# A two-layer hybrid decoder trunk: the projection for the state-space mixer is handed out ahead of the convolution's

## The chip, the cores and the metric

The kernel runs on one core of a Trainium2 chip. The metric is the device time of one execution in microseconds (us). Three runs of the kernel before took 914.29, 914.33 and 915.61 us, a median of 914.33 us. All arithmetic is done on two layers, a sequence of 512 tokens and a model width of 1024.

## The reference, cut to what matters

```python
for layer in range(DEPTH):                       # 2 layers
    h = rms_norm(x, norm_g[layer])
    proj = h @ w_in[layer]                       # 1024 x 5120, ten column blocks of 512
    a_u, a_g, qd, kd, vd, b_g, c_x, c_g, m_q, m_g = jnp.split(proj, 10, axis=-1)
    y_a = s5_mixer(a_u, ...)                     # complex state space, GELU, then a GLU (w_glu)
    o_b = diff_attention(rope(qd), rope(kd), vd) # 4 heads, causal, two softmaxes each
    y_c = rglru_mixer(c_x, ...)                  # width-4 causal convolution, gates, a linear recurrence
    y_m = memory_attention(m_q, rms_norm(mem), w_mem_kv[layer])   # 256 memory tokens
    mixed = concat(y_a * silu(a_g), norm(o_b) * silu(b_g), y_c * silu(c_g), y_m * silu(m_g))
    x = x + mixed @ w_out[layer]                 # 2048 x 1024
return rms_norm(x, final_norm_g)
```

The ten blocks of `proj` depend on `h` alone, so they may be computed in any order. Each mixer can start once its own blocks are there.

## The kernel before, in words

**Weights.** All weights are cut into 136 pieces of 128 x 1024 numbers. A piece is loaded by SyncE into one of two `raw` buffers, and then split into two reduced-precision halves: ScalarE rounds it to `whi` (line 166), VectorE computes `wlo = raw - whi` (line 172). TensorE multiplies each piece three times (hi by hi, hi by lo, lo by hi; lines 517 and 537), 24 matmuls of 512 columns for one piece of `w_in`. There are three `whi` and three `wlo` buffers, and the split of a piece is handed out two pieces ahead of its use (`w_use`, line 176). A full block of 512 output columns is four pieces.

**The order.** `ORDER` (line 31) names for each layer the sequence of the projections; `kv` stands for the memory's keys and values, `gl` for the GLU, the last four for the output projection. The main loop (from line 1155 on) goes through this list. The blocks `q`, `k`, `v` and `au` are computed with the tokens on the partitions (`tm_block`), the others with the channels there (`cm_block`), in two halves `u = 0, 1`.

**Streams and steps.** Beside the main loop run the mixers, as Python generators that hand out a few instructions at a time. After every 12 weight matmuls (half a piece) `tick` (line 78) advances a counter, and each generator that is due hands out its next portion. I call one advance a step. A block of four pieces is 8 steps, `kv` is 12. Counting from the start of a layer, `q k v` and their like fix when a mixer starts:

- `attention` (line 610) starts once q, k and v are there, and hands out one of 16 items (a block of 128 queries, one head) every 2 steps. Its VectorE work is a maximum, some small operations and one combination (lines 652 to 664), and a split of the queries (`ql`).
- the evacuation of `cx` (line 1187) does the convolution: three VectorE operations for each of four column groups. After it `lru` (line 724) starts: for each of four groups a split (`xh`, `xl`), six matmuls with the four gate matrices `bh`, `bl` (lines 740 to 742), then products, a square root and a scan (lines 747, 754, 760).
- `s5` (line 927) starts after `au`: four steps that transpose u to `U`, then for each of four groups f of state columns, every 7 steps (`D_S5`, line 55): `states` (matmuls into the PSUM tile `sc`), `turned` (line 1017: six table products and six products that rotate the states, five tiles `u tcq tsq xr0 xr1`), `scans` (line 1046), `w_rows`, `turned_back`, `c_weights`, `w_turn`. It ends with four steps that make `yhi` and `ylo`, which `gl` needs: at `gl` the main loop joins the stream (line 1250).
- gates (`cg bg ag mg`) are evacuated by ScalarE and VectorE (lines 719, 720).

**What else sets the order.** The instructions of an engine are placed by a planner at build time, with what was handed out first having priority. Buffers of one pool are given out in the order in which their first writers were handed out. The pools that matter: 14 large tiles (`big`, line 97: whole activations such as `kT`, `U`, `xc`, the gates), 10 small tiles of 2 KB a partition (`sm2`, line 99: every working tile of attention, `lru` and `s5`), and in PSUM four `acc`, two `tp` and one `sc`; `sc` is shared by the scores of both attentions and by `states`. The gate matrices of `lru` occupy four small tiles from their loading on; `lru_load` (line 1126, GpSimd DMAs) is called when `cx` is at most two items ahead (`BD_AHEAD`, line 52).

Of the kernel before, what the change touches and what calls it, by code (L numbers as in the profile page):

```python
# [27 lines left out]
ROPE_THETA = 500000.0  # L28


ORDER = ["q v k kv cx au cg bg mq ag mg gl oAM0 oAM1 oBC0 oBC1".split(),
         "q k cx v kv au mq bg mg ag cg gl oAM0 oAM1 oBC0 oBC1".split()]

C_ID, C_DM, C_IF, C_KEEP, C_CM, C_END = 0, 128, 144, 152, 152, 280

# [55 lines left out]
def tile_kernel(ctx: ExitStack, tc: tile.TileContext, A, out):  # L91
# [127 lines left out]
    for l in range(DEPTH):  # L219
        for n in ORDER[l]:  # L220
            if n == "kv":
# [900 lines left out]
    def run_split(g, R):  # L1122
        for _ in split_mixed(R[{"A": "ag", "B": "bg", "C": "cg", "M": "mg"}[g]], R, g):
            pass
# [24 lines left out]
    def s5p_start(l):  # L1149
        s5_load(l, Rl[l])  # L1150
        st.start("s5p", s5_params(l, Rl[l]))
# [3 lines left out]
    for pi, (l, n, u, ids) in enumerate(plan):  # L1155
# [118 lines left out]
        if n == "o":  # L1274
            pair, half = u[:2], int(u[2])
            tile_of = {"A": "ag", "B": "bg", "C": "cg", "M": "mg"}
            waits = {"A": ("s5",), "B": ("bfin", "attn"), "C": ("cfin", "lru"), "M": ("mem",)}
            first = "o" + u == ORDER[l][-4]
            if first:
# [6 lines left out]
            for g in pair:  # L1286
                if half == 0 and g not in R:
                    st.join(*waits[g])
                    run_split(g, R)
            if half == 1 and "o" + u == ORDER[l][-3]:  # L1290
                def nextsplit(R=R, gs=ORDER[l][-2][1:3]):
                    for g in gs:
                        while any(w in st.live for w in waits[g]):
                            yield
                        yield from split_mixed(R[tile_of[g]], R, g)
                st.start("nextsplit", nextsplit())
            if "o" + u == ORDER[l][S5P_AT - 4] and l + 1 < DEPTH:
                s5p_start(l + 1)
            if "o" + u == ORDER[l][-2]:
                st.join("nextsplit")  # L1300
# [74 lines left out]
```

## Time and profile before

| | |
|---|---|
| median of three runs | 914.33 us |
| the profiled execution's own time | 913.18 us |
| its span (first to last instruction of the program) | 911.4 us |
| TensorE busy (matmul) | 890.5 us, 98% of the span |
| TensorE weight loads | 748.9 us, 82% |
| VectorE busy | 658.8 us, 72% |
| ScalarE busy | 509.6 us, 56% |
| GpSimd busy | 42.1 us, 5% |
| granted TensorE clock | 0.998 |
| HBM traffic | 88.6 MB, 97 GB/s |

The share of an engine over the span is a mean over stages with different limits; the stretches below are read one by one. A matmul's recorded duration is longer than the distance to the next matmul's start, since matmuls overlap in the array, so busy TensorE is not TensorE at its peak.

### The profile page before, as it was taken

What the parts mean: (1) busy time and instruction counts of PE and PEld (TensorE: products, weight loads), DVE (VectorE), ACT (ScalarE), POOL (GpSimd) and SP (SyncE); (2) the same over time, 40 slices, a digit from 0 to 9 for tenths busy, and PEclk for the clock granted to TensorE, in tenths of its full rate; (3) what the DMA queues carried; (4) which work ended last, traced back from release to release, by engine and by line L of the source; (5) the groups of instructions that cost most, each with busy time, mean ns of one, the idle gap of its engine ahead of it and who ended that gap; (6) DMA issues with size and microseconds to landing.
All of it is one profiled execution on the core that took longest, in us unless ns stands there. A gap on an engine that the chain in (4) does not pass through costs nothing.

```text
span 911.4 us, 12490 instructions
## 1 busy us (share of the span) xinstructions
PE 890.5 (98%) x4542; PEld 748.9 (82%) x4542; DVE 658.8 (72%) x1315; ACT 509.6 (56%) x1031; POOL 42.1 (5%) x86
## 2 busy tenths in 40 slices
PE   8999999999999999999999999999999999999996
PEld 5788888978878888888888888898888888788885
DVE  6985888678999856983474667764899996666343
ACT  6764887985434265922554568766655344863133
POOL 1001000001110100000100000000101110000000
PEclk9999999999999999999999999999999999999999
DMA  5733432212222237432343332432112222152322
GB/s 185 196 118 102 140 93 70 70 47 72 75 70 61 75 104 205 135 111 93 127 140 92 93 93 70 137 95 70 51 47 83 63 74 93 47 185 98 108 72 93
DMA packets 80930, 90.07 MB, mean 99 GB/s; under 512 B 23778, under 2 KB 58211, under 8 KB 80868
## 3 DMA queue, kind: packets, MB, share of 16 engines
q1 hardware_dynamic: 77842, 85.72, 30.3%
q10 hardware_dynamic: 722, 2.36, 0.8%
q0 software_dynamic: 2304, 1.18, 0.5%
q8 instruction: 36, 0.59, 0.3%
q14 instruction: 26, 0.21, 0.1%
HBM read 84.40 MB, written 4.19 MB: 97 GB/s over the span
## 4 chain that ended last, share of the span: by engine, by line
PE 72%; DVE 18%; ACT 6%; issue 2%; DMA 1%; SPq 0%; DVEq 0%; ACTq 0%
PE acc L537 37%; PE acc L517 17%; PE acc L1261 5%; DVE wlo L172 2%; DVE u L347 2%; DVE xr L1046 2%; DVE wt L347 2%; PE ms L682 1%; DVE xr L347 1%; PE tp L312 1%; PE sc L810 1%; PE tp L1012 1%; PE sc L647 1%; PE sc L648 1%; ACT whi L166 1%
## 5 line engine op out<-in xcount | busy, mean ns | idle before, releaser
L172 DVE TENSOR_TENSOR wlo<-raw,whi 128x1024 fp32r<-128x1024 f32 x136 | 166.2, 1222 | 125.3 <-ACT whi L166 121.6
L166 ACT CAST whi<-raw 128x1024 fp32r<-128x1024 f32 x136 | 143.1, 1052 | 194.1 <-PE acc L537 120.1
L517 PE MATMUL acc<-hThi,whi 128*128 128x512 f32 x384 | 154.3, 402 | 0.0
L517 PE MATMUL acc<-hThi,wlo 128*128 128x512 f32 x384 | 151.1, 394 | 0.0
L517 PE MATMUL acc<-hTlo,whi 128*128 128x512 f32 x384 | 150.6, 392 | 0.0
L537 PE MATMUL acc<-whi,hThi 128*128 128x512 f32 x256 | 104.1, 407 | 1.0 <-ACT whi L166 1.0
L537 PE MATMUL acc<-wlo,hThi 128*128 128x512 f32 x256 | 100.7, 393 | 0.0
L537 PE MATMUL acc<-whi,hTlo 128*128 128x512 f32 x256 | 100.7, 394 | 0.0
L537 PE MATMUL acc<-wlo,mxh 128*128 128x512 f32 x256 | 100.2, 391 | 0.0
L537 PE MATMUL acc<-whi,mxh 128*128 128x512 f32 x256 | 100.1, 391 | 0.0
L537 PE MATMUL acc<-whi,mxl 128*128 128x512 f32 x256 | 100.1, 391 | 0.0
L517 PEld LDWEIGHTS acc<-hThi,wlo 128*128 128x128 f32 x384 | 72.2, 188 | 15.0
L517 PEld LDWEIGHTS acc<-hTlo,whi 128*128 128x128 f32 x384 | 72.4, 189 | 13.4
L517 PEld LDWEIGHTS acc<-hThi,whi 128*128 128x128 f32 x384 | 72.4, 189 | 13.0
L537 PEld LDWEIGHTS acc<-whi,hThi 128*128 128x128 f32 x256 | 56.3, 220 | 9.1 <-ACT whi L166 1.4
L537 PEld LDWEIGHTS acc<-whi,hTlo 128*128 128x128 f32 x256 | 56.1, 219 | 7.8 <-DVE hTlo L315 0.2
L537 PEld LDWEIGHTS acc<-wlo,hThi 128*128 128x128 f32 x256 | 56.4, 220 | 7.1
L537 PEld LDWEIGHTS acc<-whi,mxl 128*128 128x128 f32 x256 | 48.1, 188 | 9.8
L537 PEld LDWEIGHTS acc<-wlo,mxh 128*128 128x128 f32 x256 | 48.1, 188 | 9.7
L537 PEld LDWEIGHTS acc<-whi,mxh 128*128 128x128 f32 x256 | 48.1, 188 | 9.6
L982 POOL DMA_DIRECT2D MT<-kq x64 | 32.1, 509 | 490.7 <-DVE kq L347 339.4
L658 ACT ACTIVATE e<-sc,nmx 128x128 f32<-128x128 f32 (+3 forms) x64 | 33.1, 524 | 7.1 <-DVE nmx L654 5.8
(316 smaller groups left out, 1642.2 us busy)
## 6 DMA issues: line engine op xcount, KB each, us to landing
raw<-in_w_in_dram SPq DMA_DIRECT2D x80, 512.0 KB, 3.7
raw<-in_w_out_dram SPq DMA_DIRECT2D x32, 512.0 KB, 3.3
raw<-in_w_mem_kv_dram SPq DMA_DIRECT2D x16, 512.0 KB, 3.3
x<-in_x_dram SPq DMA_DIRECT2D x8, 512.0 KB, 4.7
raw<-in_s_w_glu_dram SPq DMA_DIRECT2D x16, 256.0 KB, 3.1
mt<-in_mem_dram SPq DMA_DIRECT2D x4, 512.0 KB
xd<-x SPq DMA_DIRECT2D x4, 512.0 KB, 4.0
x<-xd SPq DMA_DIRECT2D x4, 512.0 KB, 5.6
```

Of the source, the lines that this page charges most:

```text
L166: S.copy(hi, wbuf[j])
L172: V.tensor_tensor(out=lo, in0=raw, in1=hi, op=ALU.subtract)
L312: lastins["pe"] = PE.transpose(pt[:, k, :], h[:, kk * 128:(kk + 1) * 128], ident)
L347: V.tensor_tensor(out=o, in0=a, in1=b, op=op)
L517: PE.matmul(a[j][:, :ncol], w[:, kk, c], h(k), start=(hf == 0 and i == 0), stop=(hf == 1 and i == 3 * nh - 1))
L537: PE.matmul(a[t], h(k, t), w[:, kk, :], start=(p == 0 and kk == 0 and i == 0), stop=(p == np_ - 1 and kk == 1 and i == 2))
L647: PE.matmul(s[:, m, :M], qh[:, m, h, :], kT[m][:, h, :M], start=True, stop=False)
L648: PE.matmul(s[:, m, :M], ql[:, m, h, :], kT[m][:, h, :M], start=False, stop=False)
L658: S.activation(e[:, m, :N], s[:, m, :N], AF.Exp, bias=nmx[:, m:m + 1], scale=0.125, accum_out=sm[:, m:m + 1])
L982: G.dma_start(out=MT[g * 64 + 64 - n:g * 64 + 64, g, t], in_=kq[g * 64:g * 64 + n])
L1046: V.tensor_tensor_scan(out=xr_[i][:, j, :], data0=dec, data1=xr_[i][:, j, :], initial=0.0, op0=ALU.mult, op1=ALU.add)
L1261: PE.matmul(a, w[:, k, s, j * 128:(j + 1) * 128], h[:, 2 * hf + k, :], start=(hf == 0 and i == 0), stop=(hf == 1 and i == 5))
```

## The change

```diff
-ORDER = ["q v k kv cx au cg bg mq ag mg gl oAM0 oAM1 oBC0 oBC1".split(),
-         "q k cx v kv au mq bg mg ag cg gl oAM0 oAM1 oBC0 oBC1".split()]
+ORDER = ["q v k kv au cx cg bg mq ag mg gl oAM0 oAM1 oBC0 oBC1".split(),
+         "q k v kv au cx mq bg mg ag cg gl oAM0 oAM1 oBC0 oBC1".split()]
```

In the first layer `au` and `cx` change places. In the second layer `cx` moves from the third place to the one behind `au`, so `v`, `kv` and `au` each come one block (8 steps) sooner. Nothing else differs: the same pieces are loaded and multiplied, and the same mixers run. The steps at which the mixers' portions are handed out, counted from the start of each layer, follow from the code:

| portion | layer 1 before | after | layer 2 before | after |
|---|---|---|---|---|
| attention, items 0 to 15 | 25 to 55 | 25 to 55 | 33 to 63 | 25 to 55 |
| `cx` (convolution) | 36 to 44 | 44 to 52 | 16 to 24 | 44 to 52 |
| `lru`, gate matmuls | 45 to 48 | 53 to 56 | 25 to 28 | 53 to 56 |
| `lru`, the rest | 49 to 58 | 57 to 66 | 29 to 38 | 57 to 66 |
| `s5`, `U` | 53 to 56 | 45 to 48 | 53 to 56 | 45 to 48 |
| `s5`, first `w_rows`, first `turned` | 57, 59 | 49, 51 | 57, 59 | 49, 51 |
| `s5`, last `scans` | 82 | 74 | 82 | 74 |
| `s5`, `yhi` complete | 89 | 81 | 89 | 81 |
| memory attention, from | 93 | 93 | 77 | 77 |
| `gl`, from | 92 | 92 | 92 | 92 |

## Rows read from the trace of the kernel before

**Rows 1.** The page: busy us (share of span), engine by engine.
```profile
PE 890.5 (98%) x4542; PEld 748.9 (82%) x4542; DVE 658.8 (72%) x1315; ACT 509.6 (56%) x1031; POOL 42.1 (5%) x86
```
**Rows 2.** Busy time by stretch: us from the start, length, each engine's busy us (instructions).
```profile
117.00:147.00 30.00, 29.55 (x158) 24.65 (x157) 25.08 (x48) 21.88 (x61) 0.00 (x0) 1.00 0.36 106
147.00:184.00 37.00, 37.00 (x184) 34.51 (x184) 25.43 (x42) 32.59 (x68) 0.00 (x0) 1.00 0.18 57
184.00:207.00 23.00, 21.98 (x125) 17.87 (x124) 17.93 (x27) 17.70 (x32) 0.00 (x0) 1.00 0.16 47
207.00:303.00 96.00, 94.00 (x517) 80.03 (x517) 92.10 (x175) 40.57 (x84) 16.04 (x32) 1.00 0.25 75
303.00:335.00 32.00, 31.26 (x157) 26.01 (x156) 21.89 (x40) 15.76 (x21) 0.00 (x0) 1.00 0.26 83
...
593.00:643.00 50.00, 49.72 (x259) 45.37 (x259) 29.57 (x52) 32.00 (x76) 0.00 (x0) 1.00 0.24 74
643.00:750.00 107.00, 106.07 (x608) 90.31 (x607) 102.42 (x196) 54.34 (x122) 16.05 (x32) 1.00 0.22 68
```
**Rows 3.** The same, for the weight split on VectorE (line 172) alone.
```profile
207.00:303.00 96.00, 14.64 (x12) 1.00 0.25 75
643.00:750.00 107.00, 14.57 (x12) 1.00 0.22 68
```
**Rows 4.** The chain of waits between 207 and 303 us, shares by line.
```profile
by line: DVE u L347 14.0%; DVE wlo L172 10.9%; DVE wt L347 10.3%; DVE xr L347 8.4%; DVE xr L1046 7.7%; issue 6.9%; DVE tcq L347 5.2%; DVE xp L347 4.7%; PE acc L517 4.7%; DVE tsq L347 4.1%; DVE VV L347 3.0%; DVE bg L720 2.7%; DVE cg L765 2.4
```
**Rows 5.** TensorE instructions in time: start us, duration us.
```profile
187.90 0.83 PE L682 MATMUL ms<-v,pT 128*128 128x128 f32 x6
...
223.11 0.39 PE L517 MATMUL acc<-hThi,whi 128*128 128x512 f32 x1
223.34 0.39 PE L517 MATMUL acc<-hTlo,whi 128*128 128x512 f32 x1
...
726.64 1.59 PE L810 MATMUL sc<-kv,qm 128*128 128x256 f32 x12
```
**Rows 6.** VectorE instructions in time, inside the state-space part.
```profile
281.99 0.67 DVE L347 TENSOR_TENSOR wt<-apr,bbx 128x512 f32<-128x512 f32 x1
282.58 0.69 DVE L347 TENSOR_TENSOR wt<-api,bby 128x512 f32<-128x512 f32 x1
```
**Rows 7.** Groups of instructions, both layers: convolution, recurrence; busy us, mean ns.
```profile
L1187 DVE SCALAR_TENSOR_TENSOR xc<-cx,pv,xc 128x509 f32<-128x509 f32 (+2 forms) x24 | 18.0, 749 | 3.4 <-ACT xc L1185 3.0
L760 DVE TENSOR_TENSOR_SCAN li<-lr,xc 128x512 f32<-128x512 f32 x8 | 9.6, 1212 | 0.0
L747 DVE SCALAR_TENSOR_TENSOR xc<-li,xc 128x512 f32<-128x512 f32 x8 | 5.5, 691 | 2.6 <-ACT li L743 2.5
L347 DVE TENSOR_TENSOR xl<-xc,xh 128x512 fp32r<-128x512 f32 x8 | 5.5, 686 | 0.5 <-ACT xh L735 0.5
L754 DVE SCALAR_TENSOR_TENSOR li<-a,li 128x512 f32<-128x512 f32 x8 | 5.4, 686 | 1.5 <-ACT a L753 1.4
L347 DVE TENSOR_TENSOR xc<-xc,li 128x512 f32<-128x512 f32 x8 | 5.3, 682 | 4.5 <-ACT li L756 4.5
```
**Rows 8.** Attention's VectorE groups between 147 and 207 us.
```profile
L652 DVE TENSOR_REDUCE mx<-sc 128x2 f32<-128x1024 f32 (+1 forms) x6 | 6.8, 1133 | 3.5 <-PE sc L650 3.5
L664 DVE SCALAR_TENSOR_TENSOR e<-e,cc 128x512 f32<-128x512 f32 (+1 forms) x7 | 4.9, 694 | 0.2
L347 DVE TENSOR_TENSOR ql<-qT,qh 64x512 fp32r<-64x512 f32 x4 | 2.7, 685 | 0.1
L663 DVE TENSOR_SCALAR cc<-sm,nlam,rc 128x1 f32<-128x1 f32 x7 | 1.9, 270 | 0.2
```
**Rows 9.** The reduction of memory attention, both layers.
```profile
L812 DVE TENSOR_REDUCE mmx<-sc 128x4 f32<-128x1024 f32 x8 | 9.8, 1223 | 4.9 <-PE sc L810 4.9
```
**Rows 10.** Tile U between 150 and 330 us: its writer, first and last start.
```profile
L935 ACT COPY U<-tp x4: 562/603/638, 196.2 to 202.8; 128x512 f32<-128x512 f32 x4
```
**Rows 11.** Loads on the queues: count, KB each, median us from issue to landing.
```profile
raw<-in_w_in_dram SPq DMA_DIRECT2D x80, 512.0 KB, 3.7
bd<-in_lru_w_a_dram POOLq DMA_DIRECT2D x4, 64.0 KB, 2.3
```

## The prediction

> **What bounds the kernel now.** I read the page's busy shares first, then the stretches, then the chain of waits of one stretch. The shares say TensorE: 98% busy against 72% of VectorE [rows 1]. The stretches show that this hides two regimes. From 147 to 184 us TensorE is busy all the time and VectorE only 25.43 of 37 us. From 207 to 303 us VectorE is busy 92.10 of 96 us, and from 643 to 750 us 102.42 of 107 [rows 2]. These two stretches are steps 57 to about 83 of the layers, the state-space part from its first `w_rows` to its last `scans`. That TensorE also reads as busy there is no contradiction: matmuls of 512 columns start 0.227 us apart and are recorded as 0.39 us long [rows 5], so a waiting matmul is stretched. What counts is how many weight pieces get through: 12 pieces in 96 us and 12 in 107 [rows 3], 8.0 and 8.9 us a piece, where 24 matmuls at 0.227 take 5.45. The rest is other matmuls: 517 in all less 12 x 24 = 288 is 229, at about 0.12 (six in 0.83 us is 0.14, twelve of 256 columns in 1.43 is 0.12 [rows 5]) some 27 us, so TensorE needs about 65 + 27 = 92 of the 96 us. Both engines are near full, VectorE is the one that ends last: the chain of this stretch runs over its lines (u, wlo, wt, xr, tcq, xp, tsq, VV), and TensorE's line 517 has 4.7% of it [rows 4]. So, in this part of each layer, VectorE work added costs its own length, and TensorE work added costs little; outside it is the other way round.
>
> **The change, part by part.**
>
> *Loads.* The same pieces go through SyncE's queue; of the eight loads of `au` and `cx` in layer 1 four go ahead of the other four, all 512 KB and 3.7 us to landing against 5.45 us of use [rows 11]. In layer 2 the four of `cx` move behind twelve others. Cost 0; the two `raw` buffers hide it, and an uncovered load would cost 3.7 us once. GpSimd's `bd` loads are handed out one item later in layer 1, six later in layer 2; they land in 2.3 us [rows 11] and are wanted 21 steps later, about 80 us. Cost 0.
>
> *Start of the state-space part.* It moves 8 steps ahead in both layers; its end too (step 81 instead of 89), and `gl` at step 92 joined it without waiting before, so nothing is gained at that join. The work itself is unchanged: 0. What changes is its company.
>
> *Company, layer 1.* Before, the convolution, the recurrence and nearly all of attention were over at step 57, under stretches in which VectorE had 11.6 and 5.1 us idle [rows 2]. After, the stretch is steps 49 to 75 and takes in, per layer:
> - the recurrence (steps 53 to 66). Its five groups sum to 9.6 + 5.5 + 5.5 + 5.4 + 5.3 = 31.3 us for two layers, 15.65 for one [rows 7]. Recorded durations overlap: two operations of 128x512 start 0.59 us apart and last 0.67 [rows 6], so VectorE is held for 0.88 of the sum, 13.8 us. About 1.2 us (one scan) lay in the stretch already: 12.6.
> - the convolution's last two column groups: 6 operations of 0.749 [rows 7], times 0.88: 4.0.
> - attention's items 12 to 15, the widest: 1.13 + 0.69 + 0.27 and two small ones of about 0.16, 2.4 us an item; with four `ql` of 0.685 x 0.88 [rows 8] it is 9.7 + 2.4 = 12.1.
>
> Sum on VectorE: 28.7 us. TensorE's part of the same portions also leaves earlier, TensorE-bound steps: per item 4 score matmuls (0.9 us) and 8 transposes and products of 0.13 (1.05), about 2.0, four items 8.2; the recurrence's 24 gate matmuls at 0.227, 5.4. So the earlier steps get 13.6 us shorter and the stretch 28.7 longer: +15.1.
>
> *Company, layer 2.* Attention also comes 8 steps sooner, so its last items overlap the state-space part as before: 0. The recurrence moves in from steps 25 to 38: +13.8. The convolution's half: +4.0. Out of the stretch goes the first head of memory attention (steps 77 on): a reduction of 1.22 [rows 9], two small operations, three of 128x512, together 3.6. Net on VectorE +14.2. TensorE: the gate matmuls leave the block of `v`, -5.4; the memory head's matmuls (about 3.7, of which the scores 1.43 [rows 5]) are now paid in TensorE-bound steps, +3.7. Sum +12.5.
>
> *What softens it.* The two stretches leave VectorE 3.9 and 4.6 us idle [rows 2]; if the added work fills them, 27.6 becomes 19. If the idle time is start-up (the chain's first link waits for other engines), it stays. I take the middle, 23 us. A backlog on VectorE can be carried by at most the two pieces by which splits are ahead (11 us); before, the last rotations ended after 303 us as well, so this allowance is already used.
>
> *U.* Its four copies ran from 196.2 us [rows 10], three steps after their turn; they waited among others for a large tile. After, at step 45, a tile is free. Worth 0 to the path, since the next portion (step 57) was on time; at most 4 us, the delay of one step.
>
> *Sum.* 913.18 + 23 = 936.2 us for an execution like the profiled one, which lies 1.15 us below the median of the runs; so 937 us. With the softening at either end, 933 to 942; with an error of a third in the amounts, 925 to 950.
>
> **The rivals.**
>
> *Much slower: ten small tiles.* At the first `turned` (step 51) these are wanted at once: four gate matrices of the recurrence (until step 56), two `xp`, and `u tcq tsq xr0 xr1`: eleven, and the pool has ten. Before, the gate matrices were gone by step 48. Given out in the order of the code, the eleventh would wait for work that itself needs small tiles later. So either the recurrence gets ahead or the rotation holds `sc` for about five steps, and the scores of attention with it. For it: the count. Against it: the planner may find an order that I don't see, and no row shows such a wait. Price: five steps of 4 us (96 us over 24 steps [rows 2, 3]) are 20 us in each layer if all of it shows, so up to 937 + 40 = 977; with half of it 957. It decides from the point where TensorE's four `acc` are full, two blocks later. A milder form pushes the state-space part back five steps and takes away part of my sum.
>
> *No change.* If splits of weights were always let through ahead of the rotations, TensorE would set the pace throughout, and its work is the same: 98% busy [rows 1] leaves nothing to win, and 914 us stays. Against it: 8.0 us a piece where VectorE is full [rows 3].
>
> *Faster.* The earlier start lets rotations run in VectorE's idle time: 11.6 + 5.1 us in layer 1, 20.4 us in layer 2 from 593 to 643 [rows 2]. If the planner spreads the work evenly, the stretches become TensorE-bound. The gain is then what TensorE loses there: 96 - 92 = 4 us in layer 1 and, by the same sum (288 x 0.227 + 320 x 0.12 = 104 of 107), 3 in layer 2, with U's step at most 11: 903 to 907 us. Against it: the idle time of layer 1 lies before step 57, and what moves there is not only the state-space part, since convolution and recurrence move out of it into the full steps.
> The Trainium skill (Perfetto Trace Analysis, section Optimization Strategy) says that a kernel whose most contended engine changes over time may gain when such regimes are interleaved; by that rule this change, which starts the VectorE-heavy part under attention, should come out at this rival's time. The rows agree that there are two regimes; they also show that the part moved out of the light regime is VectorE work too, so I give the rule this rival's chance only.
>
> *It does not do what it says.* The planner could place the instructions much as before. It did follow the order handed out (U at 196.2 us [rows 10] is step 55), so I count this under no change.
>
> **How the numbers follow.** 0.2% (1.8 us) is about what a measurement of this kernel can tell from no change. My forecast has 0.52, the ten tiles with more than 950 us 0.18, no change 0.12, faster 0.18. Slower by over 0.2% is then 0.70, within 0.2% 0.12, faster 0.18. The forecast's own range is 925 to 950 us. Taking in no change, half of the faster cases, and half of the much slower ones gives 905 to 962.
>
> **What would show it.** In the changed profile VectorE should be full from the first `w_rows` on for about 120 us in each layer, with fewer than 12 pieces split in each 96 us; the scans of line 760 should lie between those of line 1046; TensorE should run its last gates (steps 80 to 92) at 5.5 to 6 us a piece with VectorE under 60% busy. ScalarE, busy 40.57 us there now, can take over at most the 32.59 us of the stretch from 147 to 184 [rows 2], 73 of 120, so it should not be the bound. The forecast is wrong if the pieces get through that stretch at 8 us each, if attention's scores stand behind `sc` for several steps, or if the late gates are no faster than before.

## The result, and the profile after

The changed kernel takes 960.75 us (median of 4 runs, 959.98 to 961.55), the kernel before 914.67 us (914.29 to 915.61): ratio 1.0502, 95% interval 1.0484 to 1.0521. It is 46.1 us slower, where 23 were forecast. The profiled execution has a span of 959.1 us and a mean granted clock of 0.975; before, 911.4 us and 0.998.

First the page's busy shares (us, share of the span, instructions), which answer to [rows 1]:
```profile
PE 907.1 (95%) x4542; PEld 757.1 (79%) x4542; DVE 658.7 (69%) x1315; ACT 517.4 (54%) x1035; POOL 42.0 (4%) x86
```
Hardly any work came on top: VectorE has 658.7 us in 1315 instructions, before 658.8; TensorE has the same 4542 matmuls; ScalarE has four instructions more, loads of its function tables at 1.28 us each. The same work was arranged worse. The view of what TensorE (PE) waited for says where; its columns are the line that waited, the writer that ended the wait, us in all, number of waits, the longest:
```profile
PE acc L517 <- DVE bg L720: 15.7, 2, 13.6
PE acc L517 <- DVE wlo L172: 10.1, 4, 6.7
PE sc L810 <- ACT me L818: 5.6, 2, 3.5
```
Before, no wait of TensorE was longer than 2.3 us. Two of these name VectorE (DVE): a gate that it had not yet taken out of `acc`, and a piece that it had not yet split. The third is memory attention, whose scores waited for ScalarE's exponentials.

The stretches, in the columns of [rows 2] (PE, PEld, DVE, ACT and POOL busy, the granted clock, the DMA share, GB/s):
```profile
184.00:216.00 32.00, 30.93 (x145) 23.63 (x143) 28.25 (x48) 15.46 (x30) 0.00 (x0) 1.00 0.21 66
216.00:240.00 24.00, 23.45 (x134) 19.43 (x134) 17.38 (x35) 16.88 (x35) 4.00 (x8) 1.00 0.09 26
240.00:259.00 19.00, 17.56 (x103) 14.83 (x101) 18.85 (x38) 14.41 (x20) 2.59 (x6) 1.00 0.10 30
259.00:279.00 20.00, 13.31 (x50) 10.09 (x48) 20.00 (x35) 5.29 (x13) 1.42 (x3) 0.83 0.19 57
279.00:305.00 26.00, 22.22 (x119) 18.68 (x119) 23.03 (x43) 10.89 (x27) 4.00 (x8) 0.87 0.21 63
322.00:355.00 33.00, 33.00 (x149) 27.30 (x149) 13.35 (x22) 19.64 (x32) 0.00 (x0) 1.00 0.34 111
703.00:718.00 15.00, 14.59 (x82) 12.29 (x80) 14.85 (x35) 13.80 (x20) 0.97 (x2) 1.00 0.02 5
718.00:734.00 16.00, 2.48 (x20) 2.29 (x20) 15.97 (x23) 2.37 (x4) 4.00 (x8) 0.65 0.13 38
734.00:767.00 33.00, 32.94 (x166) 27.73 (x167) 32.47 (x65) 12.72 (x29) 4.01 (x8) 0.91 0.22 67
799.00:811.00 12.00, 5.93 (x25) 5.35 (x26) 4.13 (x7) 9.01 (x27) 0.00 (x0) 0.60 0.14 44
811.00:839.00 28.00, 28.00 (x124) 23.06 (x124) 14.84 (x22) 15.06 (x29) 0.00 (x0) 0.93 0.24 75
```
Read the DVE column from the top. Between 184 and 240 us VectorE idles for 10.4 of 56 us; then it is full, 20.00 of 20 and 15.97 of 16 us, and just there TensorE stands still (13.31 of 20, 2.48 of 16). From 799 to 811 TensorE has 5.93 of 12 us while VectorE is busy for 4.13 us only: that is another cause. In and after each gap the granted clock is low, and 28 us of full TensorE work at 0.93 come behind the last one. An estimate of what the clock costs beside the waits' 31.4 us, at most, in the three stretches behind the gaps: 28 x 0.07 + 33 x 0.09 + 26 x 0.13 = 8.3 us. Matmuls inside the gaps come on top: two groups of twelve scores took 2.60 and 2.93 us there (800.95 and 807.10 below), where such a group took 1.59 before [rows 5].

The same view for the weight split (VectorE busy, pieces, clock, DMA share, GB/s) answers to [rows 3], where 12 pieces came in each of 96 and 107 us:
```profile
216.00:312.00 96.00, 7.30 (x6) 0.93 0.14 42
679.00:775.00 96.00, 9.73 (x8) 0.91 0.14 42
...
322.00:355.00 33.00, 7.35 (x6) 1.00 0.34 111
784.00:839.00 55.00, 7.34 (x6) 0.88 0.22 67
```
Six and eight pieces in 96 us. For the last gates it is six in 33 us, 5.5 us each, in layer 1, but six in 55 us, 9.2 us each, in layer 2, where the gap from 799 to 811 us lies.

What VectorE had in hand while TensorE stood from 718 to 734 us, from its instructions in time (start us, duration us):
```profile
717.96 1.29 DVE L347 TENSOR_TENSOR xc<-xc,li 128x512 f32<-128x512 f32 x2
719.17 2.33 DVE L760 TENSOR_TENSOR_SCAN li<-lr,xc 128x512 f32<-128x512 f32 x2
721.42 1.20 DVE L172 TENSOR_TENSOR wlo<-raw,whi 128x1024 fp32r<-128x1024 f32 x1
722.54 0.68 DVE L347 TENSOR_TENSOR tcq<-tab,tab 128x512 f32<-128x512 f32 x1
...
731.59 1.21 DVE L760 TENSOR_TENSOR_SCAN li<-lr,xc 128x512 f32<-128x512 f32 x1
732.72 0.67 DVE L347 TENSOR_TENSOR xr<-xr,u 128x512 f32<-128x512 f32 x1
733.30 1.28 DVE L720 SCALAR_TENSOR_TENSOR bg<-th,acc 128x512 f32<-128x512 f32 x2
```
The recurrence's products and scans (`xc`, `li`) and a rotation (`tcq`, `xr`) stand ahead of the gate's evacuation (`bg<-th,acc`) in VectorE's queue. Until 733.30 all `acc` are full. By its steps (57 to 66) the recurrence was to be over shortly before: this wait comes when 68 steps of the layer's weight matmuls are through. It ended some 12 us into the wait, on a VectorE that was behind. In layer 1 its four scans, by line (duration min/median/max, first and last start), stand first before, then after:
```profile
L760 DVE TENSOR_TENSOR_SCAN li<-lr,xc x4: 1203/1215/1218, 198.0 to 206.5; 128x512 f32<-128x512 f32 x4
```
```profile
L760 DVE TENSOR_TENSOR_SCAN li<-lr,xc x4: 1212/1218/1219, 255.6 to 269.1; 128x512 f32<-128x512 f32 x4
```
They come 58 to 63 us later, where eight steps at 4 us would be 32. The other thing to see is the first rotation of layer 1, on VectorE:
```profile
188.14 0.69 DVE L347 TENSOR_TENSOR xr<-sc,tcq 128x512 f32<-128x512 f32 x1 [0.90 <-PE ms L682]
188.75 0.68 DVE L347 TENSOR_TENSOR u<-sc,tsq 128x512 f32<-128x512 f32 x1
189.47 0.69 DVE L347 TENSOR_TENSOR xr<-xr,u 128x512 f32<-128x512 f32 x1
190.19 1.37 DVE L1046 TENSOR_TENSOR_SCAN xr<-mag,xr 128x128 f32<-128x128 f32 x4
191.60 0.69 DVE L347 TENSOR_TENSOR xp<-xr,tcq 128x508 f32<-128x508 f32 x1
192.20 0.68 DVE L347 TENSOR_TENSOR xp<-xr,tsq 128x508 f32<-128x508 f32 x1
192.80 1.22 DVE L172 TENSOR_TENSOR wlo<-raw,whi 128x1024 fp32r<-128x1024 f32 x1
193.94 0.68 DVE L347 TENSOR_TENSOR xr<-sc,tcq 128x512 f32<-128x512 f32 x1
```
In the code `xr0` and `xr1` are both written from `sc` before any scan. Here four scans and both products of `xr0` (190.19 to 192.20) stand ahead of the first write of `xr1` (193.94): `xr1` has no tile until `xr0` is finished with. This is the eleventh tile of the rival. Layer 2 shows the same: four scans from 655.94, the first write of `xr1` at 659.69. The convolution's last evacuation is late too (the writes of `cx`, first and last start):
```profile
L1181 ACT COPY cx<-acc x4: 586/587/589, 159.2 to 199.1; 128x512 f32<-128x512 f32 x4
```
Its matmuls were over at 184.0 us; it ran at 199.1, and it needs a small tile as well.

### The profile page after: what moved, and what is told of

The parts are those of the page before. It is cut to its first block, busy times and chain, and to the rows that moved or that the text cites. A ratio compares the mean times of both kernels' runs of the same rounds, so it can differ in the third digit from the quotient of the medians.

```text
span 959.1 us, 12486 instructions
## 1 busy us (share of the span) xinstructions
PE 907.1 (95%) x4542; PEld 757.1 (79%) x4542; DVE 658.7 (69%) x1315; ACT 517.4 (54%) x1035; POOL 42.0 (4%) x86
## 4 chain that ended last, share of the span: by engine, by line
PE 68%; DVE 18%; ACT 9%; issue 2%; DMA 2%; SPq 1%; DVEq 0%; ACTq 0%
PE acc L537 33%; PE acc L517 18%; PE acc L1261 5%; DVE u L347 2%; DVE wlo L172 2%; DVE xr L347 2%; DVE xr L1046 2%; PE ms L682 1%; DVE wt L347 1%; PE sc L647 1%; PE sc L810 1%; ACT whi L166 1%; DVE xp L347 1%; PE sc L648 1%; PE tp L312 1%
## 5 line engine op out<-in xcount | busy, mean ns | idle before, releaser
L517 PE MATMUL acc<-hThi,whi 128*128 128x512 f32 x384 | 157.1, 409 | 16.4 <-DVE bg L720 15.7
L517 PE MATMUL acc<-hThi,wlo 128*128 128x512 f32 x384 | 154.7, 404 | 10.1 <-DVE wlo L172 10.1
L517 PE MATMUL acc<-hTlo,whi 128*128 128x512 f32 x384 | 153.5, 400 | 0.0
L517 PEld LDWEIGHTS acc<-hThi,wlo 128*128 128x128 f32 x384 | 74.2, 193 | 27.1 <-DVE wlo L172 11.7
```

Of the source, the lines that this page charges most:

```text
L517: PE.matmul(a[j][:, :ncol], w[:, kk, c], h(k), start=(hf == 0 and i == 0), stop=(hf == 1 and i == 3 * nh - 1))
```

## The experiments

Differences are medians less that of the kernel before run with them (914.3 to 914.9 us).

**One layer at a time.** `ORDER` with the new line for one layer, the old one for the other.

> Only layer 1 takes the new order, layer 2 keeps the old one. Theory A, crowding (the forecast's: VectorE work of the recurrence, the convolution and attention's last items is paid in the state-space stretch): layer 1's share of the forecast, +11 to +15, so 925 to 930 us. Theory B, ten small tiles (the first rotation finds no tile for xr1, the planner runs xr0's scans first, the convolution's evacuation and the recurrence get late, and their work then piles up on VectorE): the share that the trace of the changed kernel shows when gl starts, +20, so 932 to 937 us.

Measured 932.66 us, +18.1.

> Only layer 2 takes the new order. Theory A, crowding: +8 to +12.5, so 922 to 927 us. Theory B, ten small tiles: the rest of the 46 us, +24 to +28, so 938 to 943 us. With the run that changes layer 1 alone the two differences should add up to 46 within 5 us if the layers do not touch each other.

Measured 941.40 us, +26.8. The sum is 44.9 of 46.1: the layers cost on their own, and layer 2 costs more, although less was forecast for it. Both runs lie in the ranges of theory B (ten small tiles), which says little: those ranges were read off the changed kernel's own trace, and the next runs show that these tiles are the smaller part.

**Eleven small tiles.** The room came from set-up values moved into a table that is written later, and from small buffers that now share a name:
```
-    sm2 = ctx.enter_context(tc.tile_pool(name="sm2", bufs=10))
+    sm2 = ctx.enter_context(tc.tile_pool(name="sm2", bufs=11))
...
-    dt = c32("dt")
+    dt = t32()        # a slice of tab0
...
```

> The changed kernel with eleven small tiles in place of ten; the room comes from values of the set-up phase that now lie in a table not yet in use, nothing is left out. In its program xr1 is written ahead of xr0's scans again. Theory A, crowding: 955 to 962 us, as the changed kernel, for VectorE has the same work in the same steps. Theory B, ten small tiles: the wait is gone, 935 to 942 us, what the forecast gave for crowding alone. If it comes out under 925 us, crowding costs little by itself.

Measured 950.44 us, +35.9: 10.2 us of the 46.1 went. In the first rotation of layer 1 on VectorE both writes now come first:
```profile
187.07 0.68 DVE L347 TENSOR_TENSOR xr<-sc,tcq 128x512 f32<-128x512 f32 x1
...
190.00 0.68 DVE L347 TENSOR_TENSOR xr<-sc,tcq 128x512 f32<-128x512 f32 x1
190.60 0.68 DVE L347 TENSOR_TENSOR xr<-xr,u 128x512 f32<-128x512 f32 x1
...
191.94 0.42 DVE L1058 TENSOR_TENSOR_SCAN xr<-mag,xr 128x128 f32<-128x128 f32 x1
```
So the clash is real, and neither theory is enough: most of the loss stays.

> The kernel before with eleven small tiles, laid out as in the eleven-tile run of the changed kernel. If the eleventh tile helps only where eleven are wanted at once: 912 to 916 us. If more small tiles are good for any order: 905 us or less, and then the 10 us of the eleven-tile run say nothing about the change.

Measured 913.61 us, ratio 0.9995 (0.9985 to 1.0004). The eleventh tile and its new layout are worth nothing without the clash.

> The changed kernel with eleven small tiles, and the low halves of the recurrence's gate matrices left out, so that two more tiles are free; that takes away 16 matmuls and 4 subtractions in the whole run, some 4 us at most. Theory A, crowding: 946 to 950 us. Theory B, with eleven tiles still too few because the convolution and the recurrence need tiles besides: 930 to 941 us.

Measured 944.41 us, 5.8 less than with eleven tiles alone, of which up to 4 is the work left out. It lies between the two expectations; more tiles than eleven are worth at most some 6 us. The convolution's last evacuation came at 189.2 us there and at 198.2 with eleven tiles, so it had been waiting for one more tile; the recurrence's scans still began at 248.1, so tiles are not the main thing that makes them late.

**The state-space part held back.** Eight `yield`s ahead of `yield from s5(l, R)`.

> The changed kernel with the state-space part held back eight steps in both layers, so that it runs at the steps that it had before, while the convolution and the recurrence stay late. Eleven tiles are then never wanted at once, for the gate matrices are gone by step 56 and the first rotation comes at step 59. Theory A, crowding: of the recurrence's 13.8 us two thirds still lie beside the state-space part in each layer, the convolution and attention no longer, so 922 to 931 us. Theory B, ten small tiles: 914 to 921 us.

Measured 933.12 us, +18.5, above both ranges. The state-space part is at its old steps here, and the recurrence comes eight steps late. The 18.5 us are near 2 x 2/3 x 13.8 = 18.4, the whole held length of what lies beside it, with nothing off for the gate matmuls that left TensorE's earlier steps; but that was fitted afterwards, and the lower clock has a part in it (the mean granted clock is 0.990, before 0.998).

**The recurrence's work on VectorE.** In `lru` the five VectorE groups go:
```
-            tt(xl, xc[:, c, :], xh, ALU.subtract)
+            xl = xh
...
-            V.scalar_tensor_tensor(out=xc[:, c, :], in0=i_[:, c, :], ...
...
-            V.scalar_tensor_tensor(out=i_[:, c, :], in0=a2, ...
...
-            tt(xc[:, c, :], xc[:, c, :], i_[:, c, :], ALU.mult)
-            V.tensor_tensor_scan(out=i_[:, c, :], ...
```

> The changed kernel with eleven small tiles and all of the recurrence's VectorE operations of 128x512 left out (15.65 us by recorded durations in each layer, 13.8 held); its matmuls and ScalarE work stay, the subtracted half is replaced by the half that is there. Theory A, crowding: the recurrence is most of what was added, 920 to 930 us. Theory B, tiles: the waits stay, 940 to 950 us.

> The kernel before with all of the recurrence's VectorE operations of 128x512 left out, as in the run of the changed kernel without them, which lost 28 us by it. Theory A, crowding (that work costs its length only beside the state-space part): before, it lay in steps 45 to 58 under TensorE's work, so 912 to 915 us. If VectorE's work costs everywhere: 886 to 900 us.

Measured 922.11 us (+7.8), 28.1 less than with eleven tiles, as theory A had it; and 911.38 us, only 3.5 less than before, just under theory A's range and far from the other one. The same work costs 24.6 us more in its new place. TensorE's waits for `bg` and `wlo` are gone from the list of its waits; what leads it is the other cause:
```profile
PE sc L815 <- ACT me L823: 5.9, 2, 3.9
```

**The end of the state-space part.** In layer 2, after the change, ScalarE writes `yhi` from 783.9 us and `mpT` of memory attention's first head only at 810.1; before, `mpT` at 773.7 came ahead of `yhi` at 782.7. Both are large tiles, of which there are fourteen. TensorE's instructions in time show the heads' scores one behind the other, each waiting for `sc`:
```profile
798.48 0.39 PE L517 MATMUL acc<-hThi,wlo 128*128 128x512 f32 x1
800.95 2.60 PE L810 MATMUL sc<-kv,qm 128*128 128x256 f32 x12 [2.08 <-ACT me L818]
807.10 2.93 PE L810 MATMUL sc<-kv,qm 128*128 128x256 f32 x12 [3.55 <-ACT me L818]
810.59 0.79 PE L517 MATMUL acc<-hThi,whi 128*128 128x512 f32 x1 [0.56 <-DVE ag L720]
```
Only when the last head has read `qm` does `mpT` get a tile. The edit holds the last portion back:
```
         outputs(3)
-        yield
+        for _ in range(9):
+            yield
         yhi = b8([P, 4, L], "yhi", F32R)
```

> The changed kernel with the last portion of the state-space part, which writes yhi and ylo, held back eight steps in both layers, to the steps of the kernel before. Theory C, large tiles (in layer 2 yhi and ylo take the large tiles ahead of mpT, so the heads of memory attention cannot go on and their scores run one behind the other, TensorE idle from 799 to 811 us): 948 to 952 us, and mpT of the first head is written before yhi again. If the 12 us are only late work of VectorE: 958 to 962 us.

Measured 951.68 us, +36.8: 9.3 us went. `mpT` starts at 785.4 us there, and the wait for `me` is gone from the list.

> The changed kernel with eleven small tiles and with yhi and ylo held back eight steps; nothing is left out. Both clashes of tiles are gone and only the crowding is left, which is what the forecast's 23 us were for. If the causes add up (10.3 for the small tiles, 8 to 9 for the large): 941 to 943 us, crowding 27. If the small tiles and the large ones cost partly the same time: 945 to 950 us. If the forecast's size of crowding was right: 937 us.

Measured 941.75 us (941.22 to 942.63), +27.1, ratio 1.0295 (1.0281 to 1.0309). The two clashes add up, 10.2 and 8.8 us, and 27.1 are left for crowding. TensorE's waits name it, and three stretches (columns as in [rows 2]) show what comes with it, the lower of the two clock levels (1.2 and 2.4 GHz), with TensorE busy for 14.1 us in all:
```profile
PE acc L527 <- DVE bg L730: 12.8, 2, 10.5
PE acc L527 <- DVE wlo L172: 8.2, 3, 5.6
```
```profile
263.60:270.50 6.90, 3.40 (x8) 2.75 (x9) 6.90 (x14) 0.00 (x0) 0.00 (x0) 0.51 0.25 78
277.30:284.10 6.80, 5.54 (x15) 4.38 (x16) 5.67 (x14) 1.57 (x5) 0.00 (x0) 0.50 0.25 77
717.60:731.30 13.70, 5.13 (x12) 4.06 (x13) 13.67 (x25) 2.14 (x3) 0.00 (x0) 0.50 0.15 45
```

> Eleven small tiles, the recurrence's VectorE operations left out, and yhi and ylo held back eight steps: all three causes taken away from the changed kernel at once. If small tiles, crowding by the recurrence and large tiles are the whole of the 46 us: 910 to 915 us. If something else of the new order costs as well: 918 us or more.

Measured 913.91 us, -1.0. Its stretch answers to those of 259 to 279 us above, with TensorE at 19.43 in place of 13.31 us and the clock at 1.00:
```profile
259.00:279.00 20.00, 19.43 (x119) 16.39 (x118) 19.40 (x38) 12.03 (x33) 0.74 (x2) 1.00 0.17 54
```
Against the kernel before with the same work left out (-3.5) 2.5 us remain. The account: 10.2 (small tiles) + 8.8 (large tiles) + 24.6 (the recurrence beside the state-space part) + 2.5 (all else) = 46.1. The sum comes out by construction, for each term is the difference of two of these runs; what the runs show is that all else is only 2.5 us, and that the large tiles cost about the same with ten small tiles (9.3), with eleven (8.8) and with the recurrence's work left out besides (8.8).

What the 24.6 us are made of was not taken apart. They hold more than VectorE's time: the lower clock in the three stretches above, at most half of 14.1 us (an estimate), while the stretch shown here has 1.00; and perhaps tiles, since two more than eleven gave up to 5.8 us.

**The recurrence late instead.** It waits for the state-space part's end and loads its gate matrices then.

> The changed kernel, but the recurrence starts only when the state-space part is over (step 81 in place of 53), and its gate matrices are loaded then, so that neither its VectorE work nor its four tiles lie beside the state-space part. Theory A, crowding: only the convolution's half and attention's last items are left of the sum, 914 to 925 us. Theory B, ten small tiles, is met by this as well: 914 to 930 us. A third theory, that the early state-space part is itself what costs (its splits and gates wait for it in any company): 935 to 955 us.

Measured 929.35 us, +15.1, with TensorE's waits for `bg` and `wlo` gone and that for `me` at 5.6 us. That is above theory A's range, inside theory B's, and below the third, which falls. Of the 15.1 us the large tiles, still clashing here, are about 8.8; so by this estimate the early state-space part and the very late recurrence together cost some 6 us.

> The changed kernel, the recurrence started only when the state-space part is over, and yhi and ylo held back eight steps; nothing is left out. Crowding by the recurrence's place: with the late recurrence alone 929.4, less the 8 to 10 us of the large tiles in layer 2, 919 to 922 us. If the recurrence costs its length wherever it stands: 938 us or more.

Measured 929.26 us (927.09 to 933.07), +14.6: a miss. The edit did two things. The recurrence waits for the state-space part's end, and that end is what was held back, so the recurrence came eight steps later still, among memory attention and the splits of the first out-projection, where layer 1 lost what layer 2 gained: TensorE's scores waited 5.9 us there for ScalarE's exponentials, which stood behind the recurrence's square root and a split, and 2.1 us for VectorE's part of a split. It shows that a later place is not free; it does not tell the recurrence's place from its work better than the runs above.

**Looking for a faster version.** First layer 2 as `q k cx v au kv mq ...`.

> The kernel before, with the state-space part's u ahead of the memory's keys and values in layer 2, and behind the convolution and v, so that the recurrence (steps 25 to 38) and the state-space part (from step 41) do not lie together. Theory A, crowding: attention lies beside the state-space part from its start, as VectorE work of 9 to 12 us, but the heads of memory attention no longer do: 910 to 920 us. Theory C, large tiles: yhi and ylo come before memory attention begins, so there is no clash, within the same 910 to 920 us; with a clash 925 to 930 us.

Measured 933.43 us, +18.5, above both ranges: a miss. TensorE's longest group of waits there is for `sc` behind attention's exponentials, 6.8 us in 4; why attention and the state-space part get in each other's way there was not followed up, so the account above holds for this change and does not price another order. Then the splits:
```
-                V.tensor_tensor(out=lo, in0=raw, in1=hi, op=ALU.subtract)
+                e_ = G if (30 <= j < 44 or 98 <= j < 112) and j % 2 == 0 else V
+                e_.tensor_tensor(out=lo, in0=raw, in1=hi, op=ALU.subtract)
```

> The kernel before, with seven of the subtractions that write wlo in each layer's state-space part (every second piece) done by GpSimd, which takes 17 us off VectorE there. Crowding says that VectorE's length is paid there until TensorE is the bound, 4 us in layer 1 and 3 in layer 2: 904 to 910 us. If GpSimd slows VectorE down or is too slow for the pieces: 916 us or more.

> As the run before this one, with every fourth piece instead (three or four in each layer, 8 us off VectorE): 907 to 912 us by crowding; if GpSimd's way costs more than it gives, half of what the run with every second piece loses.

Measured 937.81 us (+23.2) and 923.87 us (+9.2), both slower, the second by somewhat less than half of the first; a section below says what the trace shows. No version that does all of the work beat the kernel before.

## Why the prediction missed, and what it had right

The measured 960.75 us lie above the forecast's range of 925 to 950. The way was right; the steps that failed are the two clashes of tiles, one set aside as a rival and one put at nothing (19.0 us together), and the terms of the company, whose sum came out near by luck.

**What bounds the kernel, and the direction.** Right. Time on VectorE beside the state-space part is paid at about its length: 28.1 us for the recurrence's VectorE work there (2 x 13.8 = 27.6 held), 3.5 in its old place. One reading does not hold, that a waiting matmul is stretched: the matmul at 798.48 above lasts 0.39 us like the others, and the next waits 2.08 us. The count of pieces, on which the argument rests, does not need it. The twelve scores that the sums take at 1.43 us stand in [rows 5] at 1.59; that changes little.

**Company.** The size was near: 23 us forecast, 27.1 measured with the clashes gone. Its terms were not. The recurrence was put at 15.6 net (12.6 + 13.8 less twice 5.4 for TensorE); it cost 24.6. That TensorE did not keep what it saved earlier, because it then stood with its `acc` full, is argued and not shown: the clock, at most 7.0 us by the estimate above, had no term in the prediction and could cover most of the 9.0 between the two. Convolution and attention were put at some 12 net; with the recurrence out, 2.5 were left. The two errors cancel, which is luck: the 27.6 before softening are nearly the 27.1 measured. The softening did not come: VectorE has its idle time at 184 to 240 us, ahead of the backlog, and waits for ScalarE's part of the recurrence (`li` and `xh`) for 7.0 of the 10.4 us.

**Ten small tiles.** The mechanism was named, with its count and its place; the order that came of it was neither of the two named, for the planner ran `xr0` through and `sc` was held for some 7 us (188.14 to 195.22), not five steps. The step that failed is that it was set against the forecast, as a rival, when it comes on top of it. It happens in both layers, and at 10.2 us for the two it cost half of the lower price given (20).

**Start of the state-space part.** The step "its end too (step 81 instead of 89), and `gl` at step 92 joined it without waiting before, so nothing is gained at that join. The work itself is unchanged: 0" failed. Only the join was weighed. The end also takes large tiles, and eight steps earlier it takes them ahead of memory attention. No term and no rival held these 8.8 us. Together, 937 and the two clashes give 956 of the 960.75.

**What would show it.** Scans of the recurrence between those of the rotation: yes. Late gates at 5.5 us with VectorE at 13.35 of 33 us: yes in layer 1, no in layer 2 (9.2 us). Fewer than 12 pieces in 96 us: yes. VectorE full for 120 us from the first `w_rows`: no, first idle, then full. *It does not do what it says*, *no change* and *faster* fell with the first run. With them fell what the Trainium skill (Perfetto Trace Analysis, section Optimization Strategy) would have made of it; a later sentence of that section, that gaps which repeat on the engine that should be full can mean that there is no room for the next tile, fits the gap from 799 to 811 us better, though here it comes once.

## What to carry to other kernels

When a part is moved, count the tiles that are wanted at once, pool by pool, at its new start and at its new end: with buffers given out in order, a missing one did not show here as a wait for a buffer but as a changed order, and its cost came on top of what the engines lost. Work added to a full engine cost about its length here, although another engine was relieved elsewhere; so count such relief only where something shows that it is kept. The gaps of TensorE were followed by stretches at a lower granted clock (0.87 to 0.93 here), so price the gap and what comes behind it.

## What was not expected of the hardware

GpSimd did not take time off VectorE. Its subtraction of 128x1024 took 2.66 us on average against 1.22 on VectorE, and some of VectorE's operations waited meanwhile. In the run with every second piece, GpSimd's instruction, then VectorE's:
```profile
223.74 2.40 POOL L173 TENSOR_TENSOR wlo<-raw,whi 128x1024 fp32r<-128x1024 f32 x1 [4.53 <-DVE kq L348]
```
```profile
223.66 0.68 DVE L348 TENSOR_TENSOR u<-sc,tsq 128x512 f32<-128x512 f32 x1
224.26 0.68 DVE L348 TENSOR_TENSOR xr<-sc,tcq 128x512 f32<-128x512 f32 x1
224.86 1.84 DVE L348 TENSOR_TENSOR xr<-xr,u 128x512 f32<-128x512 f32 x1
226.62 0.67 DVE L721 SCALAR_TENSOR_TENSOR cg<-th,acc 128x512 f32<-128x512 f32 x1
```
Two operations that read one input from PSUM (`sc`) took 0.68 us beside it; the one with both inputs in SBUF took 1.84 and ended just behind GpSimd's (226.14). The Trainium skill (SBUF — State Buffer, section SBUF: two separate sides) says that a VectorE instruction with two SBUF inputs contends with a GpSimd one that reads SBUF, and that the second to come is blocked until the first is through; the trace agrees. Added up, VectorE was busy for 663.2 us in that run, before for 658.8, although 14 subtractions (17.1 us) had left it: beside 11 of the 14 one of its operations lasted 0.4 to 2.2 us longer than the median of its kind, 18.0 us together. So VectorE got no relief; why the kernel lost 23 us by it stays open.

TensorE came back slowly from a gap: the first matmul of 512 columns after the gap that ends at 810.59 took 0.79 us, the ones before it 0.39, as at the lower of its two clock levels (1.2 and 2.4 GHz), and the next 28 us had a granted clock of 0.93.
